# First sums of the down weights in two half tiles, product 4 first in five blocks, transposes placed later

## The chip, the cores and the metric

The kernel runs on one core of one Trainium2 chip. The metric is device time in microseconds of one execution. A core has five engines that run side by side: TensorE (PE, matmuls and transposes into PSUM), VectorE (DVE), ScalarE (ACT), GpSimd (POOL) and SyncE (SP), which here only issues DMAs. Each works through its own list of instructions in order, and waits on semaphores where an instruction needs another engine's result.

## What is computed

A trunk of two layers on 1024 tokens of width 1024. Layer 0 mixes tokens with a chunked gMLP, layer 1 with differential attention. After each mixer come a dense MLP of width 4096 with a squared ReLU and a gated embedding. The change touches the MLP alone:

```python
def _sqrelu_mlp(x, w_up, w_down):
    return jnp.square(jax.nn.relu(x @ w_up)) @ w_down
...
    for i in range(DEPTH):
        ...                                  # h = h + _rmsnorm(m, g_mix_post[i])
        f = _sqrelu_mlp(_rmsnorm(h, g_ffn_pre[i]), f_w_up[i], f_w_down[i])
        h = h + _rmsnorm(f, g_ffn_post[i])
        gate = jax.nn.sigmoid(_rmsnorm(h, g_ple_pre[i]) @ ple_w_gate[i] + ple_b_gate[i])
```

All is float32. A float32 operand is split in two parts, a high one (rounded by ACT) and the low rest (a subtraction on DVE); this is a "cut" in the code, and each product takes three matmuls: high by high, low by high, high by low (`mm3`, L345 to L347).

## The kernel before

**Two layers of the same code.** `ffn` runs once in each layer, from about 320 us (FFN 0) and from about 1685 us (FFN 1). Both matrix products are done by the seven-product scheme of Strassen and Winograd on quarters: fewer matmuls, more sums on DVE.

**Up.** `transpose_to` turns each of the eight token tiles on PE (L296), copies it out of PSUM, and for tiles 4 to 7 forms the sums of the quarters of X (x11, x6, x21, x12; L306 to L309) and cuts them into X[3] to X[7] by L282 (high, on ACT) and L283 (low, on DVE). There are 16 blocks q of columns, each of seven products n. `load_up` loads a block's weights, sums them (L557 to L569) and cuts them (L516, L517). `block` adds up the products (L589), applies the squared ReLU (L593) and stores seven quarters of the hidden rows to DRAM. In the first five blocks (EARLY) products 1 and 2, which need only tiles 0 to 3, run ahead of the rest; the rest then runs in the order 6, 7, 5, 4, 3.

**Down.** 56 steps in four groups g: 16 steps each for g = 0, 1, 2 and 8 for g = 3. A step is 24 matmuls. `load_down` (L692) has SP load a step's weights into a tile x[0] (two quarters a1, a2) and a half tile x[1], and the hidden rows into a room; `split_down` (L713) forms two sums on DVE and cuts weights and hidden rows. `lead_l` and `lead_s` say how many steps ahead of the matmuls the program calls the two; the tiles of a group lie in a ring (`sets`), the rooms in a ring of seven. At a group's last step `evict` adds the finished PSUM banks to MA on DVE: L765 at the end of group 0, L767 and L768 at the end of group 1, L770 to L772 at the end of group 2, L774 in the last; `half` and `whole` then take the squares (L779), the gain (L780) and the norm (L784, L243, L244 on POOL), add the residual (L333), square and scale the new rows (L321, L323 on ACT) and hand four pairs of transposes to PE.

**What sets the order.** PE's list is the program's own order. The lists of the other engines come from a scheduler that models the times, so a change in one place can move instructions in others. Transposes of tiles are deferred: `whole(tt, us)` asks for them a number of microseconds after the call, counted by a tick for each matmul that the program emits.

The names in the order pieces below: pm_a_93 to pm_a_96, pb and pt are PSUM banks; xn_81 and xn_82 are the tiles xn[0] and xn[1]; hin_79, hin_80, raw and bbc are tiles that hold weights here; s_71 to s_73, xl_69/xh_67 and xl_70/xh_68 are rooms.

Of the kernel before, what the change touches and what calls it, by code (L numbers as in the profile page):

```python
# [131 lines left out]
def _trunk(ctx, tc, nc, a, out):  # L132
# [138 lines left out]
    def transpose_to(src, tt, us, gain=None):  # L271
# [19 lines left out]
        def half(hf):  # L291
            ks = quarter[hf]
            pt = ptR.next()
            for j in range(4):
                kc = hf * 4 + j
                nc.tensor.transpose(pt[:, j * P:(j + 1) * P], src[:, kc * P:(kc + 1) * P], ident)  # L296
            v = four(pt)
            if gain is not None:
                g = gcol[:, gain, ks].unsqueeze(2).broadcast_to([P, 4, P])
                x = (x21, x22)[hf]  # L300
                vec(out=x, in0=v, in1=g, op=ALU.mult)
                v = x
            if gain is None or not th:
                cut(XH[th][:, ks, cs], XL[th][:, ks, cs], v)
            elif hf:
                vec(out=x11, in0=x11, in1=x21, op=ALU.subtract)  # L306
                vec(out=x6, in0=x22, in1=x11, op=ALU.subtract)
                vec(out=x21, in0=x21, in1=x22, op=ALU.add)
                vec(out=x12, in0=x12, in1=x6, op=ALU.subtract)  # L309
                for n, v in ((6, x6), (7, x11), (4, x22), (5, x21), (3, x12)):  # L310
                    h, l = X[n]
                    cut(h[:, :, cs], l[:, :, cs], v)
# [195 lines left out]
    def ffn(i, hsrc, hdst, next_weights):  # L508
# [38 lines left out]
        def load_up(q):  # L547
# [10 lines left out]
            vec(out=t2, in0=b22, in1=b11, op=sub)  # L558
            ready(q, 6, t2)
# [9 lines left out]
            vec(out=b21, in0=b21, in1=t2, op=sub)  # L569
            ready(q, 4, b21)  # L570
            yield
# [12 lines left out]
        def block(q, steps):  # L584
# [16 lines left out]
            for n in steps:  # L601
# [7 lines left out]
                elif n == 6:  # L609
                    plus(u2, ps, t1)  # L610
                elif n == 7:
                    plus(u3, ps, u2)
                elif n == 5:
                    plus(c1, ps, u3)
                    plus(u2, ps, u2)
                    relu2(c1)
                    store((c1, 6))
                elif n == 4:
                    plus(t1, ps, u3)
                    relu2(t1)  # L620
                    vec(out=u3, in0=t1, in1=c1, op=add)
                    vec(out=c2, in0=u3, in1=h11, op=sub)
                    vec(out=t1, in0=h11, in1=t1, op=sub)
                    store((u3, 3), (c2, 1), (t1, 4))
                elif n == 3:
                    plus(u2, ps, u2)
                    relu2(u2)
                    vec(out=c4, in0=u2, in1=c2, op=sub)
                    store((u2, 2), (c4, 5))
# [31 lines left out]
        rest = (6, 7, 5, 4, 3)  # L661
# [18 lines left out]
        def cols(x, k):  # L680
# [5 lines left out]
            Ring([(x, cols(MA[:, t], 1)) for t, x in zip((0, 7, 2, 3, 4, 5), hin + xn + [raw, bbc])]),  # L686
            Ring([(x, cols(MA[:, t], 1)) for t, x in zip(range(4, 8), [raw] + hin + [bbc])]),
        ]
        steps = [(g, c) for g in range(4) for c in range(NQ if g < 3 else NQ // 2)]
# [23 lines left out]
        def split_down(n):  # L713
# [4 lines left out]
            if g == 0:  # L718

                vec(out=a2, in0=a2, in1=a1, op=sub)  # L720
                vec(out=a2, in0=x[1], in1=a2, op=sub)
                w = x[0],
            elif g == 1:

                vec(out=a2, in0=a2, in1=a1, op=sub)
                vec(out=a1, in0=x[1], in1=a1, op=sub)
                nc.sync.dma_start(cols(t4[c // 2], c % 2), a1)
                w = x[1], a2
            elif g == 2:

                vec(out=a1, in0=a2, in1=a1, op=sub)
                vec(out=x[1], in0=x[1], in1=a1, op=sub)
                nc.sync.dma_start(cols(t4[c // 2], c % 2), x[1])
                w = x[0],
# [41 lines left out]
        def half(tt, cb):  # L776
            m = cols(MA[:, tt], cb)
            ssq[tt] = small2[:, tt, :]
            act(xnR.next()[:, 0:512], m, AF.Square, accum_out=ssq[tt][:, cb:cb + 1])  # L779
# [8 lines left out]
        for m, (g, c) in enumerate(steps):  # L788
# [19 lines left out]
            if c == n_c - 1 and g == 2:  # L808
                for p in range(4):
                    half(p, 1)  # L810
                    whole(p, US_F + 2 + 4.0 * p)
# [601 lines left out]
```

## Time and profile before

| | us |
|---|---|
| median of 3 runs (lowest to highest) | 2431.13 (2425.98 to 2434.3) |
| the profiled execution | 2432.34 |
| its span on the core | 2430.6 |
| PE busy | 2338.2 (96%) |
| DVE busy | 1609.4 (66%) |
| ACT busy | 1151.7 (47%) |
| POOL busy | 235.4 (10%) |
| DMA | 441.02 MB, mean 181 GB/s |

The mean granted TensorE clock of that execution is 0.981 of full speed. Busy counts the time in which an engine executes; PE's matmuls overlap, so a busy PE is not PE at its peak. The waits of an engine name what released it, by the program's names and the line of that instruction.

### The profile page before, as it was taken

To read this page: it belongs to the slowest core of one execution; us is meant where nothing else is said; L and a number is where in the kernel's file an instruction comes from. 1 tells how busy PE (TensorE), PEld (TensorE's weight loads), DVE (VectorE), ACT (ScalarE), POOL (GpSimd) and SP (SyncE) were. 2 spreads that over 40 slices of the span, in tenths; PEclk is the share of its full clock that TensorE was granted. 3 is DMA by queue.
4 is the path that set the end of the run, shared out by engine and by line. 5 is a ranking of instruction groups with operands and counts; after the bars stand their busy time and mean duration, and the time that the engine had idled before them with its cause. 6 is when DMAs were issued, how large, how long until landed. Compare 5 with 4: busy or idle time off the path is not lost. (4 is left out here: it accounts for less than half of the span.)

```text
span 2430.6 us, 30336 instructions
## 1 busy us (share of the span) xinstructions
PE 2338.2 (96%) x10748; PEld 1933.6 (80%) x10748; DVE 1609.4 (66%) x2468; ACT 1151.7 (47%) x1929; POOL 235.4 (10%) x303
## 2 busy tenths in 40 slices
PE   9999999999999899999999989998999999979998
PEld 7888878888778677878887878777888888868787
DVE  4742698777865665563344888778877797565654
ACT  6232555555433345462224766556555554334551
POOL 1100200000000013010001342321000000000310
PEclk9999999999999899999999999999999999989999
DMA  9111445446976765244445765654544598767423
GB/s 335 47 35 53 160 143 189 154 152 216 356 246 222 243 230 174 87 160 151 145 150 184 217 176 143 156 182 136 185 149 164 177 351 275 246 222 246 173 104 121
DMA packets 200424, 441.02 MB, mean 181 GB/s; under 512 B 21040, under 2 KB 55856, under 8 KB 200144
## 3 DMA queue, kind: packets, MB, share of 16 engines
q1 hardware_dynamic: 199840, 437.89, 54.0%
q8 instruction: 85, 1.39, 0.2%
q0 software_dynamic: 432, 1.19, 0.2%
q14 instruction: 67, 0.55, 0.1%
HBM read 310.02 MB, written 133.17 MB: 182 GB/s over the span
## 5 line engine op out<-in xcount | busy, mean ns | idle before, releaser
L357 PE MATMUL pm_a<-w,xh 128*128 128x512 f32 x704 | 223.7, 396 | 1.2 <-ACT w L119 0.9
L357 PEld LDWEIGHTS pm_a<-w,xh 128*128 128x128 f32 x704 | 131.6, 189 | 29.1 <-ACT w L119 2.0
L516 ACT ACTIVATE xh<-xl 128x1024 fp32r<-128x1024 f32 x72 | 75.4, 1055 | 147.4 <-DMA xl<-hid 129.2
L357 PE MATMUL pb<-w,xh 128*128 128x512 f32 x416 | 135.9, 403 | 5.2 <-DVE gbc L950 2.9
L357 PE MATMUL pm_a<-w,xl 128*128 128x512 f32 x352 | 138.6, 394 | 0.0
L516 ACT ACTIVATE w<-ma 128x512 fp32r<-128x512 f32 x134 | 84.1, 631 | 104.6 <-PE pm_a L346 34.9
L517 DVE TENSOR_TENSOR xl<-xl,xh 128x1024 fp32r<-128x1024 f32 x72 | 87.4, 1220 | 50.7 <-ACT xh L516 50.7
L825 POOL DMA_DIRECT2D bbc<-in_ple_b_gate_dram x2 | 1.3, 627 | 1118.4 <-DVE xl L517 1118.4
L345 PE MATMUL pm_a<-xh,w 128*128 128x512 f32 x272 | 106.7, 392 | 0.0
L346 PE MATMUL pm_a<-xl,w 128*128 128x512 f32 x272 | 106.3, 391 | 0.0
L347 PE MATMUL pm_a<-xh,w 128*128 128x512 f32 x272 | 106.3, 391 | 0.0
L516 ACT ACTIVATE s<-s 128x1024 fp32r<-128x1024 f32 x56 | 58.3, 1054 | 92.3 <-DMA s<-hid 84.5
L243 POOL TENSOR_SCALAR small<-small 128x1 f32<-128x1 f32 x104 | 49.4, 475 | 543.0 <-DVE small L390 319.7
L357 PEld LDWEIGHTS pb<-w,xh 128*128 128x128 f32 x416 | 77.5, 191 | 19.6 <-DVE gbc L950 3.1
L517 DVE TENSOR_TENSOR w<-ma,w 128x512 fp32r<-128x512 f32 x134 | 91.2, 683 | 0.0
L517 DVE TENSOR_TENSOR s<-s 128x1024 fp32r<-128x1024 f32 x56 | 67.7, 1221 | 34.4 <-ACT s L516 33.6
L345 PE MATMUL pb<-xh,w 128*128 128x512 f32 x216 | 84.5, 391 | 0.0
L347 PE MATMUL pb<-xh,w 128*128 128x512 f32 x216 | 84.1, 389 | 0.0
L346 PE MATMUL pb<-xl,w 128*128 128x512 f32 x216 | 84.1, 389 | 0.0
L357 PE MATMUL pb<-w,xl 128*128 128x512 f32 x208 | 83.1, 400 | 0.0
L333 DVE SCALAR_TENSOR_TENSOR hin<-ma,small,hin 128x1024 f32<-128x1024 f32 (+1 forms) x49 | 61.6, 1260 | 28.4 <-POOL small L244 13.9
L357 PEld LDWEIGHTS pm_a<-w,xl 128*128 128x128 f32 x352 | 66.6, 189 | 13.0
(468 smaller groups left out, 7005.5 us busy)
## 6 DMA issues: line engine op xcount, KB each, us to landing
xl<-hid SPq DMA_DIRECT2D x56, 512.0 KB, 4.9
ma<-in_f_w_up_dram SPq DMA_DIRECT2D x48, 512.0 KB, 3.6
h<-hin SPq DMA_DIRECT2D x40, 512.0 KB, 3.3
hid<-ma SPq DMA_DIRECT2D x80, 256.0 KB, 2.4
s<-hid SPq DMA_DIRECT2D x40, 512.0 KB, 5.0
hin<-h SPq DMA_DIRECT2D x40, 512.0 KB, 3.4
hid<-xn SPq DMA_DIRECT2D x64, 256.0 KB, 2.8
hid<-hin SPq DMA_DIRECT2D x64, 256.0 KB, 2.8
```

Source lines behind the costliest of these rows:

```text
L243: nc.gpsimd.tensor_scalar(out=ss, in0=ss, scalar1=1.0 / n, scalar2=eps, op0=ALU.mult, op1=ALU.add)
L333: nc.vector.scalar_tensor_tensor(out=h[:, cs], in0=t_ap[:, cs], scalar=rs, in1=h[:, cs], op0=ALU.mult, op1=ALU.add)
L345: nc.tensor.matmul(ps, lhsT=lh, rhs=rh, start=start, stop=False)
L346: nc.tensor.matmul(ps, lhsT=lh, rhs=rl, start=False, stop=False)
L347: nc.tensor.matmul(ps, lhsT=ll, rhs=rh, start=False, stop=stop)
L357: nc.tensor.matmul(ps, lhsT=xs(l, kc, tt * P), rhs=r[:, cs], start=kc == 0 and k == 0, stop=kc == KC - 1 and k == 2)
L516: act(h, v, AF.Copy)
L517: vec(out=l, in0=v, in1=f32(h), op=sub)
L825: nc.gpsimd.dma_start(bbc, a["ple_b_gate"][i:i + 1, :].broadcast_to([P, D]))
```

## The change

Three edits, all in the MLP.

- *Sums in half tiles.* The first sum of `split_down` (a2 - a1) goes to a half tile of its own, one of two halves of xn[1] in turn (`sumR`), and no longer overwrites the loaded tile. The ring of group 1 has five tile pairs instead of six (xn[1] is taken out), that of group 2 has its four pairs in another order. In group 2 the weights are cut as two halves of 512 columns (t and a2) where they were one cut of 1024. The squares of `half` use xn[0] alone as a junk tile.
- *Product 4 first.* For tiles 4 to 7 the quarter x22 is cut into X[4] ahead of the four sums. In the first five blocks the weight of product 4 is made first, product 4 runs first, its result is copied by ACT into c4, and its sum with u3 follows product 7; three sums and three stores of the block come at product 5.
- *Transposes.* Those of tiles 0 to 3 in the last group are asked for at `US_F + 7` in place of `US_F + 2`, counted in the tick above.

```diff
--- before.py
+++ after.py
@@ -303,11 +303,12 @@
             if gain is None or not th:
                 cut(XH[th][:, ks, cs], XL[th][:, ks, cs], v)
             elif hf:
+                cut(X[4][0][:, :, cs], X[4][1][:, :, cs], x22)
                 vec(out=x11, in0=x11, in1=x21, op=ALU.subtract)
                 vec(out=x6, in0=x22, in1=x11, op=ALU.subtract)
                 vec(out=x21, in0=x21, in1=x22, op=ALU.add)
                 vec(out=x12, in0=x12, in1=x6, op=ALU.subtract)
-                for n, v in ((6, x6), (7, x11), (4, x22), (5, x21), (3, x12)):
+                for n, v in ((6, x6), (7, x11), (5, x21), (3, x12)):
                     h, l = X[n]
                     cut(h[:, :, cs], l[:, :, cs], v)
         for hf in range(2):
@@ -556,6 +557,10 @@
                 yield
             vec(out=b11, in0=b12, in1=b11, op=sub)
             vec(out=t2, in0=b22, in1=b11, op=sub)
+            if q < EARLY:
+                vec(out=b21, in0=b21, in1=t2, op=sub)
+                ready(q, 4, b21)
+                yield
             ready(q, 6, t2)
             yield
             if q >= EARLY:
@@ -566,9 +571,10 @@
             yield
             ready(q, 5, b11)
             yield
-            vec(out=b21, in0=b21, in1=t2, op=sub)
-            ready(q, 4, b21)
-            yield
+            if q >= EARLY:
+                vec(out=b21, in0=b21, in1=t2, op=sub)
+                ready(q, 4, b21)
+                yield
             ready(q, 3, b22)
             yield
 
@@ -610,19 +616,25 @@
                     plus(u2, ps, t1)
                 elif n == 7:
                     plus(u3, ps, u2)
+                    if q < EARLY:
+                        vec(out=t1, in0=c4, in1=u3, op=add)
+                        relu2(t1)
                 elif n == 5:
                     plus(c1, ps, u3)
                     plus(u2, ps, u2)
                     relu2(c1)
                     store((c1, 6))
+                elif n == 4 and q < EARLY:
+                    act(c4, ps, AF.Copy)
                 elif n == 4:
                     plus(t1, ps, u3)
                     relu2(t1)
+                if n == (5 if q < EARLY else 4):
                     vec(out=u3, in0=t1, in1=c1, op=add)
                     vec(out=c2, in0=u3, in1=h11, op=sub)
                     vec(out=t1, in0=h11, in1=t1, op=sub)
                     store((u3, 3), (c2, 1), (t1, 4))
-                elif n == 3:
+                if n == 3:
                     plus(u2, ps, u2)
                     relu2(u2)
                     vec(out=c4, in0=u2, in1=c2, op=sub)
@@ -658,7 +670,7 @@
             if k >= len(early) - LEAD:
                 next(loads)
             block(q, (n,))
-        rest = (6, 7, 5, 4, 3)
+        rest = (4, 6, 7, 5, 3)
         for q in range(NQ - 1):
             for n in rest if q < EARLY else rest_of:
                 next(loads, None)
@@ -683,9 +695,12 @@
         sets = [
             Ring([(MA[:, 1], cols(MA[:, 2], 0)), (MA[:, 3], cols(MA[:, 2], 1)), (raw, cols(MA[:, 4], 0)),
                   (MA[:, 5], cols(MA[:, 4], 1)), (MA[:, 6], cols(bbc, 0))]),
-            Ring([(x, cols(MA[:, t], 1)) for t, x in zip((0, 7, 2, 3, 4, 5), hin + xn + [raw, bbc])]),
-            Ring([(x, cols(MA[:, t], 1)) for t, x in zip(range(4, 8), [raw] + hin + [bbc])]),
+            Ring([(x, cols(MA[:, t], 1)) for t, x in zip((0, 7, 2, 3, 4), hin + [xn[0], raw, bbc])]),
+            Ring([(x, cols(MA[:, t], 1)) for t, x in zip((6, 5, 4, 7), [hin[1], raw, bbc, hin[0]])]),
         ]
+
+
+        sumR = Ring([cols(xn[1], k) for k in range(2)])
         steps = [(g, c) for g in range(4) for c in range(NQ if g < 3 else NQ // 2)]
         loaded, cuts, ssq = {}, {}, {}
 
@@ -717,21 +732,24 @@
                 a1, a2 = cols(x[0], 0), cols(x[0], 1)
             if g == 0:
 
-                vec(out=a2, in0=a2, in1=a1, op=sub)
-                vec(out=a2, in0=x[1], in1=a2, op=sub)
+                t = sumR.next()
+                vec(out=t, in0=a2, in1=a1, op=sub)
+                vec(out=a2, in0=x[1], in1=t, op=sub)
                 w = x[0],
             elif g == 1:
 
-                vec(out=a2, in0=a2, in1=a1, op=sub)
+                t = sumR.next()
+                vec(out=t, in0=a2, in1=a1, op=sub)
                 vec(out=a1, in0=x[1], in1=a1, op=sub)
                 nc.sync.dma_start(cols(t4[c // 2], c % 2), a1)
-                w = x[1], a2
+                w = x[1], t
             elif g == 2:
 
-                vec(out=a1, in0=a2, in1=a1, op=sub)
-                vec(out=x[1], in0=x[1], in1=a1, op=sub)
+                t = sumR.next()
+                vec(out=t, in0=a2, in1=a1, op=sub)
+                vec(out=x[1], in0=x[1], in1=t, op=sub)
                 nc.sync.dma_start(cols(t4[c // 2], c % 2), x[1])
-                w = x[0],
+                w = t, a2
             else:
                 w = f32(wl),
             cut(hh, hl, f32(hl))
@@ -776,7 +794,7 @@
         def half(tt, cb):
             m = cols(MA[:, tt], cb)
             ssq[tt] = small2[:, tt, :]
-            act(xnR.next()[:, 0:512], m, AF.Square, accum_out=ssq[tt][:, cb:cb + 1])
+            act(xn[0][:, 0:512], m, AF.Square, accum_out=ssq[tt][:, cb:cb + 1])
             vec(out=m, in0=m, in1=cols(gbc, cb), op=ALU.mult)
 
         def whole(tt, us):
@@ -808,7 +826,7 @@
             if c == n_c - 1 and g == 2:
                 for p in range(4):
                     half(p, 1)
-                    whole(p, US_F + 2 + 4.0 * p)
+                    whole(p, US_F + 7 + 4.0 * p)
                 for p in range(4):
                     half(p + 4, 1)
                 next_weights(i)
```

In the pieces below the line numbers differ from one kernel to the other: L517, L731, L732, L767, L768 and L780 of before are L518, L749, L750, L785, L786 and L798 of after; L589 is L595, L720 and L721 are L736 and L737, L323 is L324, L321 is L322, L516 is L517.

DVE at the end of group 1 (FFN 0), before; hin_80, bbc, raw and hin_79 hold the weights of successive steps of group 2:

```order
L732 TENSOR_TENSOR ma<-ma,hin_80 128x512
L517 TENSOR_TENSOR xl_69<-bbc,xh_67 128x1024
L517 TENSOR_TENSOR xl_69<-xl_69,xh_67 128x1024
L731 TENSOR_TENSOR bbc<-bbc 128x512
L732 TENSOR_TENSOR ma<-ma,bbc 128x512
L517 TENSOR_TENSOR s_72<-raw,s_72 128x1024
L517 TENSOR_TENSOR s_72<-s_72 128x1024
L731 TENSOR_TENSOR raw<-raw 128x512
L767 TENSOR_TENSOR ma<-pm_a_93,ma 128x512
L732 TENSOR_TENSOR ma<-ma,raw 128x512
L517 TENSOR_TENSOR xl_69<-hin_79,xh_67 128x1024
```

The same place after:

```order
L749 TENSOR_TENSOR xn_82<-raw 128x512
L750 TENSOR_TENSOR ma<-ma,xn_82 128x512
L518 TENSOR_TENSOR xl_69<-xl_69,xh_67 128x1024
L518 TENSOR_TENSOR s_72<-xn_82,s_72 128x512
L518 TENSOR_TENSOR s_72<-hin_80,s_72 128x512
L749 TENSOR_TENSOR xn_82<-bbc 128x512
L750 TENSOR_TENSOR ma<-ma,xn_82 128x512
L518 TENSOR_TENSOR s_72<-s_72 128x1024
L518 TENSOR_TENSOR xl_69<-xn_82,xh_67 128x512
L785 TENSOR_TENSOR ma<-pm_a_93,ma 128x512
L518 TENSOR_TENSOR xl_69<-raw,xh_67 128x512
L749 TENSOR_TENSOR xn_82<-hin_79 128x512
```

Before, a sum follows the cuts of the step before it and reads a tile cut shortly ahead; the eviction of bank 93 stands behind the sum of raw. After, the sum writes xn_82, is followed by the cuts of another step's halves, and the eviction stands behind the cut of a half.

DVE at the seam from up to down (FFN 0), before; the evictions (L589) belong to block 15, the sums (L720, L721, L725) to the groups 0 and 1:

```order
L721 TENSOR_TENSOR ma<-ma 128x512
L517 TENSOR_TENSOR s_72<-s_72 128x1024
L725 TENSOR_TENSOR xn_82<-xn_82 128x512
L589 TENSOR_TENSOR hin_80<-pb_87,hin_80 128x512
L589 TENSOR_TENSOR hin_79<-pb_87,hin_79 128x512
L517 TENSOR_TENSOR s_71<-ma,s_71 128x1024
L725 TENSOR_TENSOR xn_81<-xn_81 128x512
L517 TENSOR_TENSOR xl_70<-ma,xh_68 128x1024
L589 TENSOR_TENSOR gbc<-pm_a_93,hin_80 128x512
L720 TENSOR_TENSOR ma<-ma 128x512
L589 TENSOR_TENSOR hin_79<-pm_a_94,hin_79 128x512
```

After:

```order
L736 TENSOR_TENSOR xn_82<-ma 128x512
L518 TENSOR_TENSOR xl_70<-ma,xh_68 128x1024
L595 TENSOR_TENSOR hin_80<-pb_87,hin_80 128x512
L595 TENSOR_TENSOR hin_79<-pb_87,hin_79 128x512
L595 TENSOR_TENSOR gbc<-pm_a_93,hin_80 128x512
L518 TENSOR_TENSOR s_71<-ma,s_71 128x1024
L737 TENSOR_TENSOR ma<-ma,xn_82 128x512
L518 TENSOR_TENSOR xl_69<-xl_69,xh_67 128x1024
L736 TENSOR_TENSOR xn_82<-ma 128x512
L595 TENSOR_TENSOR hin_79<-pm_a_94,hin_79 128x512
L518 TENSOR_TENSOR xl_70<-xl_70,xh_68 128x1024
```

The evictions of banks 93 and 94 stand two rows apart before and five rows apart after.

ACT in group 3 (FFN 0), before; L321 and L323 square and scale a tile's new rows, L282 copies a transposed half out of PSUM, L113 and L516 cut weights:

```order
L516 ACTIVATE s_73<-s_73 128x1024 x2
L321 ACTIVATE ma,small<-hin_80 128x1024
L779 ACTIVATE xn_82,small_128<-ma 128x512
L323 ACTIVATE ma<-hin_79,small 128x1024
L323 ACTIVATE ma<-hin_80,small 128x1024
L282 ACTIVATE xh_67<-pt_88 128x4x128
L282 ACTIVATE xh_67<-pt_89 128x4x128
L321 ACTIVATE ma,small<-hin_79 128x1024
L282 ACTIVATE xh_67<-pt_88 128x4x128
```

After:

```order
L322 ACTIVATE ma,small<-hin_80 128x1024
L797 ACTIVATE xn_81,small_128<-ma 128x512
L324 ACTIVATE ma<-hin_80,small 128x1024
L322 ACTIVATE ma,small<-hin_79 128x1024
L324 ACTIVATE ma<-hin_79,small 128x1024
L322 ACTIVATE ma,small<-hin_80 128x1024
L113 ACTIVATE s_72<-s_72 128x1024
L282 ACTIVATE xh_67<-pt_88 128x4x128
L282 ACTIVATE xh_67<-pt_89 128x4x128
```

The first two L282 come straight after the scales of two tiles before, and after the scale of the third tile, a square of the fourth and an L113 cut afterwards.

## Rows read from the trace of the kernel before

**Rows 1.** PE's list of waits: what waits, for whom, us in total, times, longest.

```profile
PE pm_c L345 <- DVE ma L767: 12.7, 1, 12.7
PE pm_a L345 <- DVE ma L767: 9.5, 1, 9.5
PE pt L296 <- ACT ma L323: 8.8, 2, 4.4
PE pm_a L346 <- DVE s L283: 4.2, 1, 4.2
PE pm_a L345 <- DVE gbc L589: 4.1, 1, 4.1
PE pb L345 <- DVE ma L765: 3.1, 1, 3.1
PE pb L346 <- DVE s L283: 3.1, 1, 3.1
```

**Rows 2.** The table of stretches: from:to, length, busy (x instructions) by engine, PEclk, DMA.

```profile
740.00:760.00 20.00, 20.00 (x90) 16.57 (x89) 12.67 (x18) 8.41 (x12) 0.00 (x0) 1.00 0.61 209
807.70:817.70 10.00, 9.34 (x25) 6.93 (x26) 10.00 (x15) 5.48 (x10) 0.00 (x0) 0.58 0.51 172
2162.70:2172.70 10.00, 9.32 (x24) 6.98 (x25) 10.00 (x15) 5.79 (x11) 0.00 (x0) 0.58 0.49 170
709.90:714.90 5.00, 4.97 (x15) 3.93 (x16) 3.76 (x6) 1.76 (x4) 0.00 (x0) 0.66 0.74 220
920.20:926.20 6.00, 5.91 (x20) 4.96 (x21) 2.68 (x4) 2.35 (x5) 0.59 (x2) 0.58 0.55 175
```

**Rows 3.** DVE's timeline, end of group 1 of FFN 0: start, us, instruction [idle before <-releaser].

```profile
800.05 0.69 DVE L731 TENSOR_TENSOR bbc<-bbc 128x512 f32<-128x512 f32 x1 [1.54 <-DMA bbc<-in_f_w_down_dram]
...
801.39 1.22 DVE L517 TENSOR_TENSOR s<-raw,s 128x1024 fp32r<-128x1024 f32 x1
...
806.29 0.69 DVE L731 TENSOR_TENSOR raw<-raw 128x512 f32<-128x512 f32 x1 [1.57 <-DMA raw<-in_f_w_down_dram]
...
806.90 0.68 DVE L767 TENSOR_TENSOR ma<-pm_a,ma 128x512 f32<-128x512 f32 x1
```

**Rows 4.** SP's timeline at the same place: the issue of a weight load.

```profile
802.64 0.81 SPq L705 DMA_DIRECT2D raw<-in_f_w_down_dram  x2
```

**Rows 5.** The page's groups of instructions: busy us, mean ns | idle before, releaser.

```profile
L516 ACT ACTIVATE w<-ma 128x512 fp32r<-128x512 f32 x134 | 84.1, 631 | 104.6 <-PE pm_a L346 34.9
...
L516 ACT ACTIVATE xh<-xl 128x1024 fp32r<-128x1024 f32 x72 | 75.4, 1055 | 147.4 <-DMA xl<-hid 129.2
...
L517 DVE TENSOR_TENSOR w<-ma,w 128x512 fp32r<-128x512 f32 x134 | 91.2, 683 | 0.0
...
L517 DVE TENSOR_TENSOR xl<-xl,xh 128x1024 fp32r<-128x1024 f32 x72 | 87.4, 1220 | 50.7 <-ACT xh L516 50.7
```

**Rows 6.** DVE's timeline, end of group 0 of FFN 0.

```profile
706.78 0.69 DVE L725 TENSOR_TENSOR raw<-raw 128x512 f32<-128x512 f32 x1 [3.04 <-DMA raw<-in_f_w_down_dram]
```

**Rows 7.** DVE's timeline, seam from up to down, FFN 0.

```profile
615.68 0.68 DVE L589 TENSOR_TENSOR gbc<-pm_a,hin 128x512 f32<-128x512 f32 x1
```

**Rows 8.** DVE's timeline, start of FFN 0 and of FFN 1.

```profile
322.21 0.68 DVE L306 TENSOR_TENSOR ma<-ma 128x512 f32<-128x512 f32 x1
...
331.85 0.68 DVE L283 TENSOR_TENSOR s<-ma,s 128x512 fp32r<-128x512 f32 x1
...
1695.06 0.68 DVE L283 TENSOR_TENSOR s<-ma,s 128x512 fp32r<-128x512 f32 x1
```

**Rows 9.** POOL's timeline in group 3 of FFN 0.

```profile
910.26 7.65 POOL L243 TENSOR_SCALAR small<-small 128x1 f32<-128x1 f32 x2 [2.77 <-DVE small L784]
```

**Rows 10.** ACT's timeline at the same place.

```profile
920.90 1.15 ACT L323 ACTIVATE ma<-hin,small 128x1024 f32<-128x1024 f32 x1 [0.67 <-POOL small L244]
```

**Rows 11.** The page's DMA issues: KB each, us from issue to landing.

```profile
s<-hid SPq DMA_DIRECT2D x40, 512.0 KB, 5.0
...
hin<-h SPq DMA_DIRECT2D x40, 512.0 KB, 3.4
```

## The prediction

> **What bounds the kernel now.** I read the page's busy times first, where TensorE (PE) is busy for nearly the whole span, so only what PE waits for, and what those waits do to its clock, can pay. The list of PE's waits is next [rows 1]. The long ones belong to one part of the program, the two feed-forward layers (FFN 0 from about 320 us, FFN 1 from about 1685 us): 9.5 and 12.7 us for L767, the first eviction at the end of down group 1; 8.8 us in two waits for L323, the scale ahead of the transposes; 4.2 and 3.1 us for L283, the cuts of X at the start of a layer; 4.1 us for L589 at the seam from up to down; 3.1 us for L765, at the end of group 0.
>
> The third view is the table of stretches. At full clock PE starts 90 matmuls in 20 us [rows 2], about 0.225 us each, so 44.5 fit into 10 us. In the 10 us after the L767 waits it starts 25 and 24, at a mean granted clock of 0.58, which is the lower of its two levels (1.2 of 2.4 GHz) for most of the stretch [rows 2]. So an idle of that length is paid a second time: 19.5 x 0.225 = 4.4 us in FFN 0 and 20.5 x 0.225 = 4.6 us in FFN 1. After the 3.1 us at L765, 15 of 22.2 matmuls start in 5 us, 1.6 us lost [rows 2]. In the 6 us after the L323 wait the clock is 0.58 [rows 2]: 0.42 x 6 / 0.5 = 5 us at half speed, 2.5 us lost.
>
> **Part 1: first sums in half tiles, the L767 seam.** While PE is in the last steps of group 1, VectorE (DVE) prepares those of group 2 in the order of the first piece: cut of the whole tile, cut of the activations, sum of the next tile. The sum's tile is the one just cut. The cut of raw at 801.39 ends at 802.6 [rows 3]; SyncE (SP) issues the load into raw at 802.64 [rows 4]; the sum waits for its landing until 806.29, idle 1.57 us [rows 3]. The same stands at 800.05 with 1.54 us [rows 3], and back to 781 in three more. Two sums follow each other in 806.29 - 800.05 = 6.24 us, where PE needs 24 x 0.225 = 5.4 us for a step. DVE so falls behind 0.84 us a step (more in the rows before 790), and L767 stands behind the last sum [rows 3], though its product was there long before.
>
> The first order piece shows what goes: the sum of raw now writes a half tile, the cuts read that half tile and the other half of the loaded tile, and a tile's load is ordered two steps ahead of its use, some 10.8 us against 3.7 us from issue to sum. The idle of about 1.6 us a step goes. What is left for DVE in a step: two sums and two half cuts at about 0.60 us from start to start (a 128x512 operation lasts 0.683 us, overlapped with the next) and an activation cut at about 1.14, 3.6 us in all against 5.4. The price of cutting in halves: ACT 2 x 0.631 in place of 1.055, DVE 2 x 0.683 in place of 1.220 [rows 5], 0.2 and 0.15 us a step over 16 steps and two layers, 6.6 and 4.7 us in all. Both engines idle for longer than that in those steps, so I cost it at nothing; without the cover it would be the 6.6.
>
> What is late next: L767 and L768 alternate over eight banks, and after the change six other operations stand among these eight. That is 14 x 0.60 = 8.4 us against a step of 5.4, with some 1.7 us of lead, so the last banks come about 1.3 us late in each layer. Gain: FFN 0 9.5 + 4.4 - 1.3 = 12.6, FFN 1 12.7 + 4.6 - 1.3 = 16.0, together **-28.6 us**. Bounds: nothing is gained if DVE waits for another load in the same place (0), everything if the last banks are in time (-31.2). I take the value near the full gain, since the row that makes the wait is the load of a tile just freed, and that pair is no longer in the order.
>
> **The first down seam (L765).** There the sum at 706.78 waited 3.04 us for its load [rows 6], and L765 stood behind it. After the change L765 stands behind sums whose tiles were loaded two steps before. Gain 3.1 + 1.6 = **-4.7 us**, in FFN 0 alone; bounds 0 and -4.7.
>
> **The seam from up to down (L589).** Sums of group 0 that ran into the wide first tiles while the last up blocks were still being finished now need the two halves of xn[1], which two pieces of block 14 hold. They come after those pieces are stored. In the second order piece the eviction of bank 93 keeps its place, at 615.68 before [rows 7]. That of bank 94 stood two rows behind it, past one sum, and now stands five rows behind, past two cuts of a whole tile and two half operations: 2 x 1.14 + 3 x 0.60 = 4.1 us from start to start instead of 1.2. PE comes to that bank about a us after the first. I take +1.2 us in FFN 0, where it already waits 4.1 us [rows 1] and the clock is down anyway, and +2.8 us in FFN 1, where none of the long waits stands and a new one may pull the clock down: **+4 us**. Bounds from below -2 (the first eviction comes earlier by two operations, both layers), from above +8 (2.9 us in both, and a clock loss as at L765 in one).
>
> **Part 2: product 4 first in five blocks.** No matmul, no DVE operation is added; ACT copies one product a block, 10 x 0.63 us [rows 5] beside PE's matmuls, which I cost at nothing; uncovered it would be those 6.3 us. What moves is the cut that PE waits for at the start: in place of the sixth quarter of tile 7 it now needs the fourth, which the transposes give first, and its weight. In the new order the low half of that weight ends 18 operations after the first subtraction of tile 7, at 322.21 + 18 x 0.602 = 333.1, where the old one started its cut at 331.85 and ended it at 332.5 [rows 8]. That is about 0.8 us later in FFN 0. In FFN 1 the same count gives 1693.3, where the old cut started at 1695.06 [rows 8]: about 2.1 us earlier. Net **-1.3 us**; bounds -7.3 (both waits of L283 gone) and +2.
>
> **Part 3: transposes 5 us later.** The L323 wait of 4.4 us is GpSimd's (POOL): one pair of its small L243 operations lasts 7.65 us from 910.26 [rows 9], and ACT's scale of tile 0 waits for it. In PE's program tiles 0 to 3 now stand 24 matmuls, 5.4 us, later, so tile 0 finds its scale done. But in the third order piece ACT's first PSUM copies (L282) now stand behind the square of tile 3 and a cut of L113, and the square waits for a row tile that is loaded only after tile 1 is scaled. Tile 1's transposes need those PSUM banks. If tile 1's scale ends where it did, 920.90 + 1.15 = 922.1 [rows 10], the row tile lands 3.4 us later [rows 11], and then follow the residual (1.27), the square and the L113 cut (1.06 each), the copy and DVE's cut of the bank (0.6 and 0.7): 930.2, about 930.7 with the hand-overs. PE wants the bank 4.2 us after it starts on tile 0 at 915.9 + 5.4 = 921.3, so at 925.5: a wait of 5.2 us where the old one was 4.4, **+1.6 us** for the two layers, with the clock loss as before. Bounds: -13.8 (both waits, 8.8, and twice 2.5 us of clock) and +6 (a second dip).
>
> The rule on this place: the Trainium skill, SBUF — State Buffer, section Who interferes with whom, says that a DVE instruction with two inputs in SBUF shuts out a GpSimd instruction that reads SBUF for its whole length. The 7.65 us row agrees with it: it lies beside dense DVE work. By that rule alone the block ends with the DVE stretch and a later transpose escapes it, which is the first rival below.
>
> **Sum.** -28.6 - 4.7 + 4 - 1.3 + 1.6 = -29.0 from the profiled execution's 2432.3 us: 2403.3. That execution lies 1.2 us above the median of 2431.1, so I forecast **2402 us**.
>
> **Rivals.**
> (1) Part 3 works wholly: POOL's block has ended and ACT's copies come in time. For it: tile 0 is late by less than the 5.4 us given. Against: the order on ACT. 2402 - 1.6 - 13.8 = 2387. Chance 0.20.
> (2) The new waits at L589 and at the transposes reach their upper bounds: +4 and +4.4 more, 2410. For it: both stand at places where PE already waits. Against: half of the added operations are short. Chance 0.15.
> (3) Half of the L767 wait stays, because the activation loads stand behind tile loads in SP's queue and DVE still waits for one of the two: 2402 + 15.6 = 2418. For it: ACT also waits for hid loads of 5.0 us [rows 11]. Against: those loads are ordered steps ahead. Chance 0.10.
> (4) Slower: two half tiles let only two sums stand open, so DVE can't run ahead, SP's next tile load holds the activation load behind it, and every step lasts one whole loop: 5.0 us for hid [rows 11], 1.06 and 1.22 us for its two cuts and 0.69 for the sum, 8.0 us. Over 5.4 us a step this is 2.6 x 16 steps x 2 layers = 83 us: 2485. It decides as soon as that loop shuts every step; with two steps of lead the loop has 10.8 us, so I hold it unlikely: 0.05.
> (5) The seams' gain is eaten by stalls in the other groups, and the time stays where it is, within 0.3% (7.3 us, about what a measurement of this kernel can tell from no change): 0.04.
>
> My forecast itself holds 0.46. Cases that end below 2424 sum to 0.91; the uncertain size of the new waits and of the stalls that can come in groups 0 and 1 takes some of that. I give faster 0.89, same 0.06, slower 0.05. The range runs from rival (1) to a little over rival (3): 2386 to 2420.
>
> **What would show it.** Right: no PE wait at L767's new line over 2 us in either layer and a full granted clock there; no idle of DVE for a tile load in group 2; L765's wait gone; a wait of some 5 us at the second transposed tile with L282 as releaser; L589 waits in both layers. Wrong: DVE still idle about 1.5 us a step in group 2 on a load, PE idle spread over all steps of group 2, or a first wait at L323.

## The result and the profile after

| | before | after |
|---|---|---|
| median of five runs each, us | 2431.13 | 2414.77 (2410.22 to 2419.89) |
| profiled execution, us | 2432.34 | 2410.22 (span 2408.5) |
| PE's waits at the end of group 1, FFN 0 and FFN 1, us | 9.5 and 12.7 | 7.5 and 6.8 |

The ratio is 0.9939, 95% interval 0.9921 to 0.9958: faster, by 16.4 us in the medians. The forecast was 2402, so the sign and the range hold and the point is 13 us too low.

The lines of after that matter below: L783 is the eviction that was L765. In group 2, SP issues two tile loads at L720, the load of the second operand x[1] at L721 and that of the hidden rows at L725; L751 stores the second sum, which DVE has written into x[1], for group 3. In before these are L705, L706, L710 and L733.

First PE's list of waits after the change (waiter, released by: us in total, times, longest):

```profile
PE pt L296 <- DVE xl L283: 8.6, 3, 4.3
PE pm_a L346 <- DVE ma L785: 7.8, 2, 7.5
PE pm_c L346 <- DVE ma L785: 7.0, 2, 6.8
...
PE pm_a L346 <- ACT w L517: 3.7, 1, 3.7
...
PE pb L348 <- DVE w L518: 2.8, 1, 2.8
PE pm_a L346 <- DVE hin L595: 2.4, 1, 2.4
PE pm_a L348 <- DVE w L518: 2.3, 1, 2.3
PE pm_c L346 <- DVE hin L595: 1.6, 1, 1.6
```

Against [rows 1] the L765 wait is gone, L323 as a releaser is gone and L283 stands at the transposes in its place. The two waits at the end of group 1 are shorter, but they are still there. The table of stretches (from:to, length, busy and instructions of PE, PEld, DVE, ACT, POOL, then PEclk, DMA share, GB/s) just behind these two waits, and behind the transposes in both layers:

```profile
801.40:811.40 10.00, 9.67 (x28) 6.96 (x29) 10.00 (x17) 5.22 (x11) 0.00 (x0) 0.70 0.71 230
2142.00:2152.00 10.00, 8.89 (x28) 5.97 (x29) 10.00 (x17) 6.60 (x14) 0.00 (x0) 0.82 0.63 224
922.60:928.60 6.00, 5.96 (x23) 4.93 (x24) 1.96 (x3) 3.16 (x5) 3.60 (x2) 0.72 0.93 335
2263.40:2269.40 6.00, 5.94 (x20) 4.98 (x21) 1.99 (x4) 2.83 (x4) 3.60 (x2) 0.58 0.92 335
```

28 matmuls in 10 us where 44.5 fit is 16.5 x 0.225 = 3.7 us lost behind each wait, against 4.4 and 4.6 before.

What DVE waits for has changed. Its timeline before the end of group 1 (start, us, instruction [idle before <- releaser]), to set beside [rows 3]:

```profile
792.64 1.23 DVE L518 TENSOR_TENSOR xl<-xl,xh 128x1024 fp32r<-128x1024 f32 x1 [2.20 <-ACT xh L517]
...
794.99 0.68 DVE L749 TENSOR_TENSOR xn<-bbc 128x512 f32<-128x512 f32 x1
...
798.85 1.23 DVE L518 TENSOR_TENSOR s<-s 128x1024 fp32r<-128x1024 f32 x1 [2.46 <-ACT s L517]
...
800.60 0.68 DVE L785 TENSOR_TENSOR ma<-pm_a,ma 128x512 f32<-128x512 f32 x1
```

No sum (L749) waits for a tile any more. DVE's cut of the hidden rows (L518) does: it waits for ACT's cut of the same rows, and ACT waits for their load:

```profile
797.76 1.06 ACT L517 ACTIVATE s<-s 128x1024 fp32r<-128x1024 f32 x1 [4.11 <-DMA s<-hid]
```

Why that load is late is in SP's timeline (issues only, in the order of its queue):

```profile
791.64 0.38 SPq L751 DMA_DIRECT2D t<-ma  x1
792.12 0.38 SPq L725 DMA_DIRECT2D s<-hid  x1
796.54 0.32 SPq L721 DMA_DIRECT2D ma<-t  x1
...
797.91 0.39 SPq L751 DMA_DIRECT2D t<-ma  x1
...
802.83 0.32 SPq L721 DMA_DIRECT2D ma<-t  x1
```

The hidden rows go out at 792.12 and are wanted as soon as they land. One turn of the queue lasts 802.83 - 796.54 = 6.29 us where PE's step lasts 5.4, and the pause is ahead of L721, the load of the second operand. Its releaser, from SP's waits between 760 and 802 us:

```profile
SPq L721 <- DMA t<-ma: 21.2, 6, 4.0
```

L721 loads into a half of MA that the store L751 reads, so it waits for that store to land, and everything behind it in the queue waits too. One turn is 797.91 - 796.54 = 1.37 us of issues and 802.83 - 797.91 = 4.92 us from the store's issue to the next L721. The store takes longer to land than it did. DMA issues (KB each, median us from issue to landing), after at 780 to 800 us:

```profile
t<-ma SPq DMA_DIRECT2D x4, 256.0 KB, 4.7
```

and before at 776 to 806 us:

```profile
t<-ma SPq DMA_DIRECT2D x4, 256.0 KB, 2.0
```

### The profile page after: what moved, and what is told of

It is laid out like the page before. It is cut to its first block, busy times and chain, and to the rows that moved or that the text cites. A ratio compares the mean times of both kernels' runs of the same rounds, so it can differ in the third digit from the quotient of the medians.

```text
span 2408.5 us, 30517 instructions
## 1 busy us (share of the span) xinstructions
PE 2330.9 (97%) x10748; PEld 1927.0 (80%) x10748; DVE 1616.0 (67%) x2500; ACT 1158.0 (48%) x1971; POOL 230.8 (10%) x303
## 4 chain that ended last, share of the span: by engine, by line
PE 79%; DVE 9%; DMA 4%; ACT 4%; issue 3%; POOL 1%; SPq 0%; DVEq 0%; POOLq 0%; ACTq 0%
PE pm_a L358 10%; PE pb L358 6%; PE pm_a L346 6%; PE pm_a L348 6%; PE pm_a L347 6%; PE pb L348 5%; PE pb L347 5%; PE pb L346 5%; PE pm_c L346 5%; PE pm_c L347 5%; PE pm_c L348 5%; PE pm_c L358 3%; PE pt L347 2%; PE pt L346 2%; PE pt L348 2%
## 5 line engine op out<-in xcount | busy, mean ns | idle before, releaser
L517 ACT ACTIVATE xh<-xl 128x1024 fp32r<-128x1024 f32 x72 | 75.4, 1055 | 146.6 <-DMA xl<-hid 131.2
L517 ACT ACTIVATE w<-ma 128x512 fp32r<-128x512 f32 x134 | 84.3, 631 | 117.4 <-PE pm_a L347 39.5
L518 DVE TENSOR_TENSOR xl<-xl,xh 128x1024 fp32r<-128x1024 f32 x72 | 87.5, 1222 | 77.8 <-ACT xh L517 76.9
L517 ACT ACTIVATE s<-s 128x1024 fp32r<-128x1024 f32 x56 | 58.5, 1054 | 99.9 <-DMA s<-hid 82.5
L518 DVE TENSOR_TENSOR s<-s 128x1024 fp32r<-128x1024 f32 x56 | 68.0, 1223 | 57.4 <-ACT s L517 53.8
L518 DVE TENSOR_TENSOR w<-ma,w 128x512 fp32r<-128x512 f32 x134 | 91.4, 684 | 0.0
L243 POOL TENSOR_SCALAR small<-small 128x1 f32<-128x1 f32 x104 | 37.1, 357 | 548.4 <-DVE small L391 317.0
```

What stands on the lines that cost most here:

```text
L243: nc.gpsimd.tensor_scalar(out=ss, in0=ss, scalar1=1.0 / n, scalar2=eps, op0=ALU.mult, op1=ALU.add)
L517: act(h, v, AF.Copy)
L518: vec(out=l, in0=v, in1=f32(h), op=sub)
```

## The experiments

Each ratio is against runs of the kernel before on the same chip, with its 95% interval.

**The parts alone.** e1: the kernel before with the half tiles alone.

```
+            t = sumR.next()
-            vec(out=a1, in0=a2, in1=a1, op=sub)
+            vec(out=t, in0=a2, in1=a1, op=sub)
```

> Before with the half tiles for the first sums alone. Theory: this part carries nearly the whole gain. From the two profiles: the wait at the end of group 0 goes (3.1 us and 1.6 us of clock), the waits at the end of group 1 shrink from 9.5 and 12.7 us to about 7.5 and 7, together some 15 us, so 2416 us (2411 to 2421), and the rest of those two waits stays because SyncE's queue stands still at the load of the second operand's half tile, which waits for the store just issued from it; the hidden rows' loads behind it come late. Rival: the gain comes from product 4 first, which shifts all that follows; then this kernel lies within 5 us of before.

Measured: 2414.05 us, ratio 0.9948 (0.9924 to 0.9973). The longest PE waits at the end of group 1:

```profile
PE pm_c L345 <- DVE ma L773: 9.1, 2, 8.9
...
PE pm_a L345 <- DVE ma L773: 7.1, 2, 6.8
```

The intervals of e1 and of the whole change overlap for most of their length: the half tiles alone give about what the whole change gives, and leave waits of the same kind.

e2: product 4 first alone.

```
-        rest = (6, 7, 5, 4, 3)
+        rest = (4, 6, 7, 5, 3)
```

> Before with product 4 first in five blocks alone. Theory: only the waits at the start of the two layers move, about 0.6 us longer in the first and 2 to 4 us shorter in the second: 2429 us (2426 to 2432), no difference that can be measured. Rival: it carries half of the gain, 2423 us.

Measured: 2425.7 against 2427.1, ratio 1.0 (0.9986 to 1.0014): nothing that can be measured.

e3: the later transposes alone.

```
-                    whole(p, US_F + 2 + 4.0 * p)
+                    whole(p, US_F + 7 + 4.0 * p)
```

> Before with the transposes of tiles 0 to 3 asked for 5 us later alone. Theory: the wait for ACT's scale goes, and in its place PE waits for DVE's cut of the first transposed tile (a PSUM bank), 4 to 5 us in each layer, with the same fall of the clock: 2431 us, no difference. Rival: both waits are gone, 14 us less, 2417 us.

A single run took 2423.41 against a median of 2427.1, inside the 2419.2 to 2430.7 of before's own runs. What it shows is the releaser:

```profile
PE pt L296 <- DVE xl L283: 9.4, 3, 4.6
```

The L323 waits (2 x 4.4 us [rows 1]) are gone and this stands in their place: the wait has moved.

**The wait at the end of group 1.** The theory: SP's queue is held by L721, and the hidden rows behind it come late. All seven that follow change group 2 of the kernel after alone. e8 issues that one load from GpSimd's queue:

```
-                    nc.sync.dma_start(x[1], cols(t4[c // 2], c % 2))
+                    nc.gpsimd.dma_start(x[1], cols(t4[c // 2], c % 2))
```

> The changed kernel with one edit: in group 2 the half tile of the second operand is loaded by GpSimd's queue, not SyncE's. DVE's order is the same but for one place. Theory: what is left of the waits at the end of group 1 is SyncE's queue, which stands 4 to 4.5 us a step at that load until its own store has landed, with the hidden rows' load behind it; then hidden rows land some 4 us earlier, DVE does not wait for ACT's cut of them, and the two waits (7.5 and 6.8 us, and some 6 us of clock) fall below 2 us each: 10 to 18 us less than the changed kernel, 2400 us (2396 to 2405). Rival: the loads are late because PE frees the rooms late or because the DMA engines are full (hidden rows land in 5.5 us there); then the waits stay at 6 us or more and the time at 2415 us.

Measured: 2407.76, ratio 0.992 (0.9895 to 0.9945). PE's waits, and SP's between 760 and 802 us:

```profile
PE pm_a L346 <- DVE ma L785: 4.5, 2, 4.2
PE pm_c L346 <- DVE ma L785: 4.1, 2, 3.9
```

```profile
SPq L720 <- DVE xl L518: 11.4, 3, 4.0
```

This missed its expectation (waits below 2 us). About half of the waits is left: now the tile loads (L720) hold the queue until DVE has cut the tile they overwrite, with the hidden rows still behind them.

e9 leaves L721 on SP and issues the hidden rows from GpSimd's queue instead:

```
-                nc.sync.dma_start(f32(hl), hid[c][:, g * 1024:g * 1024 + 1024])
+                (nc.gpsimd if g == 2 else nc.sync).dma_start(f32(hl), hid[c][:, g * 1024:g * 1024 + 1024])
```

> The changed kernel with one edit: in group 2 the hidden rows are loaded by GpSimd's queue, all else stays on SyncE's. Theory: hidden rows are late because they stand in SyncE's queue behind the store of the second operand and the load that waits for it, not because PE frees the rooms late; on a queue of their own they are issued as soon as a room is free, some 9 us earlier at the end of group 1, and ACT's cut no longer waits for them there. The store and its load still turn SyncE's loop in some 6.3 us a step, so the weights' loads may become the wait: the waits at the end of group 1 fall from 7.5 and 6.8 us to between 0 and 4. Time 2396 to 2410 us. Rival (rooms or DMA bandwidth): hidden rows still land just before their cut and the waits stay at 6 us or more, 2415 us.

Measured: 2406.19, ratio 0.9908 (0.9889 to 0.9927); PE waits 1.2 and 4.4 us at L785 and L786 in FFN 0, 0.4 and 2.7 in FFN 1. GpSimd's issue, and DVE's last sum of group 1:

```profile
782.01 0.54 POOL L725 DMA_DIRECT2D s<-hid  x1 [4.90 <-PE pt L348]
```

```profile
797.72 0.69 DVE L749 TENSOR_TENSOR xn<-hin 128x512 f32<-128x512 f32 x1 [3.49 <-issue]
```

These are the rows that went out at 792.12 in after. Here they wait only for PE to leave the room, and go out 10 us earlier, so room wasn't the limit. But SP's loop around L721 still turns in 6.6 to 7.6 us, and now a sum comes late. The profile names no releaser for it; the load into hin went out at 792.43, and such loads land 5.3 us later there, about when the sum starts.

e12 takes both away from SP: e9, and L721 from ACT's queue (`nc.scalar.dma_start`).

> As the kernel with the hidden rows on GpSimd's queue, and the load of the second operand (the one that waits for the store) on ACT's queue, so that SyncE has the weights' loads and the store alone. Theory: no load is held by another's wait but ACT's own cuts, which stand behind that load for less than a step: the waits at the end of group 1 fall to 2 us or less, 2395 us (2390 to 2403). Rival: ACT now waits in the place of SyncE for the store (4.7 us) and the cuts behind it come late: waits of 4 us or more and idle spread over group 2, 2415 us or more.

Measured: 2405.19, ratio 0.991 (0.9891 to 0.9929); L785 still costs 7.0 us in FFN 0 and 2.2 in FFN 1, so this missed too (2 us or less). The hold-up went with the load to ACT, whose cut stands behind it:

```profile
791.69 0.33 ACTq L721 DMA_DIRECT2D ma<-t  x1
792.07 1.06 ACT L517 ACTIVATE xh<-xl 128x1024 fp32r<-128x1024 f32 x1 [3.81 <-DMA t<-ma]
```

e16 leaves only the store and L721 on SP: e9, and the tile loads of group 2 from GpSimd.

```
-                        nc.sync.dma_start(cols(x[0], k), down[c, k, 1])
+                        nc.gpsimd.dma_start(cols(x[0], k), down[c, k, 1])
```

> The changed kernel with the hidden rows and the weight tiles of group 2 loaded by GpSimd's queue; SyncE keeps the store of the second operand and the load that waits for it. Theory: with the hidden rows alone on that queue, what turned the loop was SyncE (6.6 to 7.2 us from store to store: some 5 us until the store has landed, then the load, two weight loads, the next store). Without the two weight loads in it the loop is the landing and the load, 5.2 to 5.6 us, about PE's step: the waits at the end of group 1 fall below 2 us in sum in each layer, 2400 us (2394 to 2405). Rival: the hidden rows, now behind weight loads that wait for DVE, come late again, and waits of 3 to 5 us stay: 2407 us.

Measured: 2403.9, ratio 0.9904 (0.9876 to 0.9932). The longest wait there is 1.2 us:

```profile
PE pm_c L346 <- DVE ma L785: 1.5, 2, 1.2
...
PE pm_a L346 <- DVE ma L785: 1.2, 3, 0.7
```

SP's queue still stands at L721, between 760 and 802 us:

```profile
SPq L721 <- DMA t<-ma: 33.2, 7, 6.5
```

The store and the load that waits for it are there, and that wait is even longer than in after, but no load of hidden rows or tiles stands behind it any more. The loads and stores are those of after, so their traffic isn't the cause; who stands behind whom is.

e18 cuts the pair itself: the store reads a tile that nothing overwrites and writes to rows that nothing reads. Group 3 then works on group 1's numbers, which is the part of the computation that it changes.

```
-                nc.sync.dma_start(cols(t4[c // 2], c % 2), x[1])
+                nc.sync.dma_start(hid[c][:, 0:512], cols(gbc, c % 2))
```

> The changed kernel with every transfer on SyncE's queue as there, but the store of group 2 writes a fixed tile to rows that nobody reads any more, so the load of the second operand no longer waits for that store (group 3 then works with group 1's numbers; the traffic is the same). Theory: the landing of that store is what holds SyncE and, through the hidden rows behind it, DVE and the eviction: waits at the end of group 1 under 2 us in each layer, 2399 us (2394 to 2404). Rival: the DMA engines' load in that stretch makes hidden rows late whatever stands in the queue: waits of 5 us or more, 2412 us or more.

Measured: 2390.0, ratio 0.985 (0.9822 to 0.9878), longest L785 or L786 wait 0.8 us. The time is below the expected 2394 to 2404, and the expectation was wrong on the traffic: the stores, tied to nothing, went out in group 0 (640 to 680 us), and the stretch 790 to 800 moved 176 GB/s against 223 in after. By itself this run doesn't separate the wait from the traffic; e16 does.

e19 computes the same result with the pair apart: L721 loads into 16 halves that are free in group 2, and the sum goes to the old ring of four.

```
+        x1R = Ring([cols(WT[j][:, s], k) for j in range(4) for s in range(2) for k in range(2)])
+        yR = Ring([cols(MA[:, t], 1) for t in (6, 5, 4, 7)])
...
-                vec(out=x[1], in0=x[1], in1=t, op=sub)
+                vec(out=y, in0=x[1], in1=t, op=sub)
```

> The changed kernel with two edits in group 2, the same result: the second operand is loaded into 16 half tiles of the weight slots, which are free in the down phase, one for each step, so no such load waits for a store; the sum is written to the old ring of four half tiles and stored from there. All transfers stay on SyncE's queue. Theory: with the load that waits for its store gone, SyncE is never held for a landing in group 2, hidden rows are issued when a room is free, and the waits at the end of group 1 fall below 2 us in each layer with no fall of the clock: against the changed kernel about 18 us less from the stretch between the seams, 2396 us (2388 to 2403). Rival: the 16 loads, which now run in group 1, make group 1 late instead (waits at the end of group 0 or in group 1 of 3 us and more), 2406 us or more.

Measured: 2408.57, ratio 0.9922 (0.9909 to 0.9936). PE's waits (L790 here is L785), then SP's between 760 and 800 us:

```profile
PE pm_a L346 <- DVE ma L790: 4.8, 2, 4.6
PE pm_c L346 <- DVE ma L790: 4.7, 2, 4.5
```

```profile
SPq L724 <- DVE s L518: 14.2, 3, 5.0
```

This missed, as e8 did: no wait for a store of group 2 is left, yet the hidden rows still stand behind tile loads that wait for DVE, which waits for hidden rows. The rival isn't it: between the end of group 0 and the end of group 1 PE's longest wait is 1.3 us. There are two links, and taking either away alone leaves about half of the waits.

e20 takes both away: e19 and e9 together.

> The last kernel (second operands in half tiles of their own, nothing waits for a store) with the hidden rows of group 2 on GpSimd's queue as well. Theory: two ties held the hidden rows in SyncE's queue, each worth about half of the waits at the end of group 1: the load that waits for its store (7.5 and 6.8 us to 4.6 and 4.5 without it) and the transfers that wait for DVE, the store itself and the weight loads, ahead of the hidden rows of two steps later. With both gone the hidden rows are issued as PE frees a room, and those waits fall below 2 us in each layer, with no fall of the clock: 2398 us (2392 to 2403), the fastest kernel here with the same result. Rival: the two edits mend the same half, and waits of 3 to 5 us stay, 2406 us.

Measured: 2399.03 (2397.57 to 2404.12), ratio 0.9893 (0.9879 to 0.9907), the fastest of those that compute the reference's result. PE's waits, DVE's timeline and the stretch:

```profile
PE pb L346 <- DVE ma L791: 1.3, 2, 0.8
PE pm_a L346 <- DVE ma L790: 1.1, 3, 0.7
```

```profile
788.15 1.22 DVE L518 TENSOR_TENSOR xl<-xl,xh 128x1024 fp32r<-128x1024 f32 x1
...
791.81 1.22 DVE L518 TENSOR_TENSOR s<-s 128x1024 fp32r<-128x1024 f32 x1
...
793.55 0.68 DVE L790 TENSOR_TENSOR ma<-pm_a,ma 128x512 f32<-128x512 f32 x1
```

```profile
790.00:800.00 10.00, 8.64 (x35) 5.93 (x34) 9.97 (x16) 6.42 (x13) 0.54 (x1) 1.00 0.92 312
```

DVE's step is 791.81 - 788.15 = 3.66 us without idle, the clock is full, and more bytes move than in after.

Over all runs the two waits at the end of group 1 are 9.5 to 14.4 us with before's sums (before, e2, e3), 6.8 to 10.4 with the half tiles (after, e1, e6), 3.9 to 4.6 with one link gone (e8, e19) and at most 1.2 in e16, e18 and e20. The last three groups lie apart, the first two overlap. As times, only e18 and e20 lie clear of after's interval.

**The transposes.** e6: the kernel after with them another 5 us later.

```
-                    whole(p, US_F + 7 + 4.0 * p)
+                    whole(p, US_F + 12 + 4.0 * p)
```

> The changed kernel with the transposes of tiles 0 to 3 asked for another 5 us later (US_F + 12 in place of US_F + 7). Theory: PE waits at the second tile's transposes for DVE's cut of the first tile's copy, which ends at 922 to 923 us whatever PE does; 5.4 us later PE finds it done, so the waits of 4.1 and 4.3 us and the fall of the clock behind them go, but the third tile's banks now hang on copies that stand behind a cut of late weights on ACT, so a wait of up to 3 us can come there: 5 to 13 us less than the changed kernel, 2406 us (2400 to 2411). Rival: the copies are placed later on ACT as well and the wait moves along unchanged, as it did from before to after: 2415 us.

Measured: 2415.49, ratio 0.995 (0.9934 to 0.9967), no better than after:

```profile
PE pm_a L346 <- DVE ma L785: 10.6, 2, 10.4
PE pm_c L346 <- DVE ma L785: 9.2, 2, 9.0
PE pt L296 <- DVE xl L283: 8.0, 5, 3.0
```

The wait at the transposes moves along again, in smaller pieces. The L785 waits came out longer than after's 7.5 and 6.8. Up to the one in FFN 0 the instructions of PE, DVE, ACT and GpSimd come in the same order in both kernels, so 10.4 in place of 7.5 is a difference between two executions, and a wait of one profile is known only to some 3 us.

## Why the prediction was right in sign and 13 us short

Term by term, in us. "Measured" is PE's wait, plus the matmuls that are missing in the stretch behind it at 0.225 us each, after less before; for product 4, the seam and the end of group 0 it is how far the same-numbered matmul behind the place came earlier, against the one ahead of it. Each is from one profiled execution, so the first row can be off by several us.

| term | forecast | measured |
|---|---|---|
| L767, end of group 1 | -28.6 | -2.7 - 6.8 = -9.5 |
| L765, end of group 0 | -4.7 | -5.0 |
| L589, up to down | +4 | -1.4 + 1.1 = -0.3 |
| product 4 first | -1.3 | +0.6 - 2.4 = -1.8 |
| transposes later | +1.6 | -1.0 - 0.3 = -1.3 |
| sum | -29.0 | -17.9 |

The two profiled executions differ by 22.1 us, the medians by 16.4, and the sum lies between them. Most of what it leaves of the 22.1 lies in parts whose code is the same: matmuls of the same number come 1.5 us later ahead of FFN 0 and gain 4.3 us between the two MLPs.

- **L767, the step that failed.** "... a tile's load is ordered two steps ahead of its use, some 10.8 us against 3.7 us from issue to sum. The idle of about 1.6 us a step goes." For the tiles it went, as after's DVE timeline shows. But order in the program was taken for time of issue. SP issues in order, L721 holds it up to 4.0 us a step for a store, and the hidden rows behind it went out 797.76 - 792.12 = 5.6 us ahead of use, about what a load of them takes (5.5 us in this stretch). DVE's step became 798.85 - 792.64 = 6.2 us, the same as before's 6.24, with another releaser. FFN 0: 7.5 + 3.7 = 11.2 in place of 9.5 + 4.4; FFN 1: 6.8 + 3.7 = 10.5 in place of 12.7 + 4.6. That is rival (3), which gave 2418. The place and the kind of wait were in it; what held the load was half right, since beside the tile loads it is a load behind a store (e8 and e19 take away one link each, e20 both). Before's own trace had this wait beside the tile's:

```profile
797.68 0.38 SPq L710 DMA_DIRECT2D s<-hid  x1
```

```profile
802.41 1.06 ACT L516 ACTIVATE s<-s 128x1024 fp32r<-128x1024 f32 x1 [4.20 <-DMA s<-hid]
```

```profile
803.50 1.23 DVE L517 TENSOR_TENSOR s<-s 128x1024 fp32r<-128x1024 f32 x1 [0.89 <-ACT s L516]
```

  The hidden rows went out 802.41 - 797.68 = 4.7 us ahead of use, not steps ahead, and DVE lost 0.9 us to them in that step beside the 1.57 us that the prediction counted.
- **The rest of that step** was sized right: "3.6 us in all against 5.4" is 3.66 in e20. There the same-numbered matmuls gain 10.3 and 14.1 us at the two ends of group 1, 24.4 of the 28.6 forecast. That e20's whole gain, 2425.49 - 2399.03 = 26.5 us, is close to the 29.0 is in part luck, since the other terms differ.
- **L765** came as forecast. **Product 4** moved in each layer the way it was forecast, and e2 shows that it is too small to be measured as a time. The prediction's subtraction was a little off: its rows give 333.1 - 332.5 = 0.6 us later and 1695.7 (the end of the cut at 1695.06) - 1693.3 = 2.4 us earlier, so -1.8, as measured, and not -1.3.
- **L589**: the new waits are there, 0.8 and 2.4 us in FFN 0 in place of 4.1, 1.6 in FFN 1 in place of 0.6. The prediction had added the delay of the second bank and left the first in its place; the first came earlier, which in FFN 0 gave back more than the second cost.
- **The transposes**: the mechanism is as forecast. The releaser is DVE's cut (L283), the last link of the chain worked out there, where the list of signs named the copy ahead of it (L282). ACT's square waits for the residual of the late row tile, its copy of the bank comes behind the L113 cut, and DVE's cut behind that:

```profile
917.96 1.28 DVE L334 SCALAR_TENSOR_TENSOR hin<-ma,small,hin 128x1024 f32<-128x1024 f32 x1 [5.32 <-DMA hin<-h]
...
921.89 1.29 DVE L283 TENSOR_TENSOR xl<-pt,xh 128x512 fp32r<-128x512 f32 x2 [2.64 <-ACT xh L282]
```

```profile
919.28 1.06 ACT L322 ACTIVATE ma<-hin 128x1024 f32<-128x1024 f32 x1 [2.51 <-DVE hin L334]
...
920.34 1.04 ACT L113 ACTIVATE s<-s 128x1024 fp32r<-128x1024 f32 x1
921.28 1.06 ACT L282 ACTIVATE xh<-pt 128x512 fp32r<-128x512 f32 x2
```

  PE waits 4.1 us in FFN 0 and 4.3 in FFN 1, where 5.2 was worked out, so the wait came out a little below the old 4.4 and not above it. Rival (1) asked for two things. Its first came: the 7.65 us block of GpSimd [rows 9] is not in after, where the longest such instruction is

```profile
902.45 3.27 POOL L244 TENSOR_TENSOR small<-small,mhalf 128x1 f32<-128x1 f32 x1
```

  Its second did not: ACT's copies still come late, and 5 us more (e6) don't change that.

## What to carry to other kernels

A load that stands early in the program is early only if nothing ahead of it on the issuing engine's queue waits. Before pricing a load as covered, walk its queue and ask of each transfer ahead what it waits for. The case here is a load into a buffer that a store, issued just before, still reads: give that load a room of its own (e20) or let nothing urgent stand behind it (e16), and put loads that depend on another engine's pace on the queue of an engine that has no work of its own there (ACT's queue only moved the wait to ACT in e12). If two links tie a loop, undoing one can leave much of the wait, here about half, so test them together before dropping the theory. And when one wait of a step is to go, look in the same trace for the others: here DVE already waited 0.9 us a step for the hidden rows.

## What the runs showed of the hardware

- A store of 256 KB lands 2.0 us after its issue in before's stretch (776 to 806 us) and 4.7 us in after's (780 to 800 us, medians). In after it goes out right behind three loads (790.28 to 791.17, the store at 791.64), in before 3.8 us behind the last transfer (791.42, the store at 795.17); that this is the reason isn't shown. The mean rate was 257 GB/s in after's stretch, and e20 moved 312 at 790 to 800 us.
- GpSimd issues a load in 0.54 us beside a DVE that is busy without a gap (e20's stretch: 9.97 of 10 us), and the loads of 512 KB land 5.2 to 6.7 us after it (medians between 760 and 800 us).
